# Gram blocks of the eight full chunks in one cluster, and a 16-column product for the meta chunk in the next projection tile's PSUM banks

## The chip, the core and the metric

The kernel runs on one core of a Trainium2 chip. The core has a matrix engine (TensorE, in the profile PE, with its weight loads as PEld), a vector engine (VectorE, DVE), a scalar engine (ScalarE, ACT), GpSimd (POOL), and queues from which transfers are issued (SyncE, SP). Matrix products land in PSUM, which has eight banks of 512 f32 columns on 128 partitions; VectorE and ScalarE move them from there to SBUF. The metric is the device time of one execution in microseconds (us); of several runs the median counts.

## What is computed

One layer of a hybrid encoder on 16 learned meta tokens and 512 real tokens: RMS norm, one input projection, an RWKV-7 recurrence on 16 heads of 64 beside a gated convolution, an output projection, and a final norm. The part that matters here is the recurrence, which is run as a chunk of the 16 meta tokens and eight chunks of 64 tokens.

```python
hn = _rmsnorm(h_res, norm_in_g[l])
P = hn @ w_in[l]                      # 528 x 2048 by 2048 x 8320
...
kk = (k * k_k[l]).reshape(bsz, L, H, N)
kk = kk / jnp.maximum(jnp.linalg.norm(kk, axis=-1, keepdims=True), 1e-12)
...
def step(S, inp):
    r_t, w_t, k_t, v_t, kk_t, b_t = inp
    sa = jnp.einsum('bhvk,bhk->bhv', S, kk_t)
    S = (S * w_t[:, :, None, :]
         - sa[..., None] * b_t[:, :, None, :]
         + v_t[..., None] * k_t[:, :, None, :])
    y_t = jnp.einsum('bhvk,bhk->bhv', S, r_t)
    return S, y_t

S, y_meta = lax.scan(step, S0, tuple(t[:N_META] for t in xs))
S, y_real = lax.scan(chunk_step, S, real)      # chunks of 64
```

The kernel computes a chunk in matrix form. For each chunk and head it needs the products of the chunk's keys (and betas) with its own queries and removal vectors, token against token, masked to the lower triangle: the Gram blocks.

## The kernel before

**Layout.** Channels lie on partitions, tokens along the free dimension. Two heads of 64 channels make a pair; there are eight pairs (0 to 7). The 528 tokens are laid out as nine chunks of 64, where chunk 0 is the meta chunk with 16 real columns and 48 of padding.

**The stream.** The input projection is 65 tiles of 128 output columns. `main` (L354) makes one tile from 16 blocks of weights, as three products each (the high and low halves of a split f32 number), over one or two column ranges of the tokens (`FULL`, `TAIL` with two, `REAL` with one): 96 products of about 256 columns, or 48 of 512. Each range has a PSUM bank of the pool `pm` (tag `main`, four banks), so the tile in work and the one before it hold them between them. When a tile is done, `scaled` (L363) on VectorE moves it out of PSUM.

**The pairs.** `prepare(i)` (L637) makes the operands of a pair, and `invert` (L844) inverts the triangles of two pairs at a time. Their products are small, so they are set between those of the stream: `fill(ns)` (L564) issues stream products worth that many nanoseconds, counted as 0.43 ns a column, before the next small products. This order of TensorE is written out by hand (L101), and the constants stand in `FW` (L43). The other engines' queues are ordered by the framework, from priorities and its own costs: `ahead()` (L596) raises a priority. Transfers that are to be issued later are put on a list by `later` (L545) with a due time that counts the stream's nanoseconds.

**The Gram blocks.** In `prepare`, the stationary operand of a chunk is `bk[hs, c, h : h + 2]` (64 channels of head h, 128 columns: two kinds of 64 tokens), the moving one `ar[hs, c]` (the same 64 channels, 128 columns: removal vectors and queries). So both heads use half of the array's rows each. The products are f32, and each appears in the profile as two records. `gram` (L692) issues both heads of a chunk, `masked` (L701) multiplies finished blocks with the triangle masks on VectorE and writes them to `gt` in SBUF. Before, it goes like this:

- `fill(FW["gram"])`, or `gram_b` for odd pairs (L689)
- a cluster of chunks 0 to 7 (L714): the four first in two banks `za` of the pool `pz` (tag `tz`, two banks), the others in `zc`, in the two single banks `misc` and `ser`
- four masks of 128x512 (L716, L717), then `fill(FW["gram2"])`
- a second cluster: chunk 8 (L721) in two `tz` banks `ze`; then the norm sums (L726, L727: 2 weight columns, 288 moving ones), of which one half lies beside chunk 8 in `ze[0]` and the other in `misc`; then the bonus sums `zb` (L729, L730) in `ser`
- two masks of 128x128 for chunk 8 (L734)

What follows in `prepare` sends the masked blocks through DRAM to the solver of the 16x16 triangles (L753 to L802, on VectorE) and to the operands of the recurrence.

The weights of the stream come by `prefetch` (L162): a transfer on SP's queue, a rounding copy on ScalarE (L158), and a subtraction on VectorE or GpSimd (L159) for the low half. The convolution's tiles (`C`, `h`, `B`, `gc`) use VectorE, ScalarE and GpSimd in turn (L426 to L462).

Of the kernel before, what the change touches and what calls it, by code (L numbers as in the profile page):

```python
# [9 lines left out]
F32 = mybir.dt.float32  # L10
# [3 lines left out]
ALU = mybir.AluOpType  # L14
# [4 lines left out]
P = 128  # L19
# [3 lines left out]
META = 16  # L23
L = SEQ + META
CH = 64
NCH = SEQ // CH + 1
LP = NCH * CH
# [13 lines left out]


FW = dict(  # L43
    evac=34, start=1062, lora=2200, gram=8000, gram_b=13500, gram2=5500, misc=2000, v=2000, vt=1000, solve=24500, more={0: 5500, 2: 2400},
    tr=3200, lev=3000, cp=4200, out=1500, begin=19500, p=2900, u=2900, s=5200, last=3700, mix=2600,
)

# [51 lines left out]
def hymba_kernel(ctx: ExitStack, tc: tile.TileContext, xt, xtok, front, w_in, w_out, pv, lup, cst, msk, gf, out):  # L99
    nc = tc.nc  # L100
# [11 lines left out]
    gmask = cs[:, C_GM : C_GM + 256].rearrange("p (h c) -> p h c", h=2)  # L112
# [14 lines left out]
    plan = [("lora", 0), ("k", 0), ("r", 0), ("B", 0), ("v", 0), ("k", 1), ("r", 1), ("v", 1), ("g", 0), ("g", 1)]  # L127
# [10 lines left out]
    N_IN = len(stream)  # L138
    stream += [w_out[0, g] for g in range(3)]
    quarters, chain, low = {}, {}, {}  # L140
    state = {"next": 0}

# [41 lines left out]
    pm = ph1.enter_context(tc.tile_pool(name="pm", bufs=4, space=PSUM))  # L186
    pz = ph1.enter_context(tc.tile_pool(name="pz", bufs=2, space=PSUM))
    pi = ph1.enter_context(tc.tile_pool(name="pi", bufs=1, space=PSUM))
# [128 lines left out]
    with tc.issue_after(head):  # L317
        nc.vector.tensor_scalar(
            out=omm, in0=pvt[:, V_MU : V_MU + 33], scalar1=-1.0, scalar2=1.0, op0=ALU.mult, op1=ALU.add
# [17 lines left out]
    def steps(ps, ranges, k4, q, ks=range(4), rs_=range(2)):  # L337
        hi, lo = quarters[q]
        for r, (a, b) in enumerate(ranges):
            if r not in rs_:  # L340
                continue
            for k in ks:
                kt = 4 * k4 + k
                w = slice(k * P, (k + 1) * P)
                for n, (ww, xx) in enumerate(((hi, xh), (hi, xl), (lo, xh))):
                    nc.tensor.matmul(  # L346
                        ps[r], ww[:, w], xx[:, kt, a:b], start=(kt == 0 and n == 0), stop=(kt == KT - 1 and n == 2)
                    )
                    yield (b - a) * 0.43

    def banks(ranges, name, pool, tag):
        return [pool.tile([P, b - a], F32, tag=tag, name=f"ps_{name}_{r}") for r, (a, b) in enumerate(ranges)]

    def main(j, ranges, name):  # L354
        prefetch(2 * j + 4)
        ps = banks(ranges, name, pm, "main")
        for k4 in range(4):
            if k4 == 1:
                prefetch(2 * j + 5)
            yield from steps(ps, ranges, k4, 4 * j + k4)  # L360
        return ps

    def scaled(ranges, ps, dst, base):  # L363
# [200 lines left out]
    def fill(ns):  # L564
        while ns > 0:
            seen = len(ready)
            t = step()
            if t is None:
                return
            ns -= t  # L570
            if len(ready) > seen:
                ns += FW["evac"]
# [23 lines left out]
    def ahead():  # L596
        return tc.high_priority(offset=AHEAD)
# [42 lines left out]
    def prepare(i):  # L640
        p = i % 2
# [35 lines left out]
        r = got["r", i]  # L677
# [8 lines left out]
        nc.scalar.activation(sq, k, AF.Square, scale=col(V_KK, i))  # L686
        sqh, sql = split(sq, f"sq{i}", LP)
        rh, rl = split(r, f"rk{i}", SEQ)
        fill(FW["gram_b" if p else "gram"])  # L689

        gt = cq.tile([P, 2, NCH, P], F32, tag=f"gt{p}", name=f"gt{i}")
        def gram(z, c, c0):  # L692
            for h, hs, ho in heads:
                nc.tensor.matmul(  # L694
                    z[h][:, c - c0],
                    bk[hs, c, h : h + 2, :].rearrange("p a s -> p (a s)"),
                    ar[hs, c].rearrange("p a s -> p (a s)"),
                    start=True, stop=True,
                )

        def masked(z, c0, c1):  # L701
            with ahead():
                for h in range(2):
                    nc.vector.tensor_tensor(
                        out=gt[:, h, c0:c1],
                        in0=z[h],
                        in1=gmask[:, h].unsqueeze(1).to_broadcast([P, c1 - c0, P]),
                        op=ALU.mult,
                    )


        za = [pz.tile([P, 4, P], F32, tag="tz", name=f"g{i}_0_{h}") for h in range(2)]
        zc = [pi.tile([P, 4, P], F32, tag=("misc", "ser")[h], name=f"g{i}_4_{h}") for h in range(2)]
        for c in range(8):  # L714
            gram(za if c < 4 else zc, c, c // 4 * 4)
        masked(za, 0, 4)  # L716
        masked(zc, 4, 8)  # L717
        fill(FW["gram2"])

        ze = [pz.tile([P, P + 288 * (1 - h)], F32, tag="tz", name=f"g{i}_8_{h}") for h in range(2)]  # L720
        gram([z[:, 0:P].unsqueeze(1) for z in ze], 8, 8)  # L721
        n2 = tr(f"n2{i}")
        zn = pi.tile([2, 288], F32, tag="misc", name=f"n2_{i}")
        zs = ((zn, 0, 288), (ze[0][0:2, P : P + 288], 288, LP))
        for z, a, b in zs:
            nc.tensor.matmul(z, ones[:, P : P + 2], sqh[:, a:b], start=True, stop=False)  # L726
            nc.tensor.matmul(z, ones[:, P : P + 2], sql[:, a:b], start=False, stop=True)  # L727
# [3 lines left out]
        with ahead():  # L731
            for z, a, b in zs:
                nc.scalar.copy(n2[0:2, a:b], z)
            masked([z[:, 0:P].unsqueeze(1) for z in ze], 8, 9)  # L734
        nc.scalar.copy(r, zb)
        fill(FW["misc"])

# [801 lines left out]
```

## Time and profile before

| what | value |
|---|---|
| three runs | 1003.79, 1004.59, 1004.99 us; median 1004.59 |
| the profiled execution | 1003.5 us, of which the span from its first to its last instruction is 1001.6 |
| mean granted clock of TensorE | 0.997 |
| input projection's products (L346) | starts from about 5 to 839 us of the span |
| Gram products (L694) | 288 records, 20.4 us busy, from 79.4 to 554 us |
| masks (L704) | 32 of 128x512 at 675 ns, 16 of 128x128 at 286 ns |

A row of a group names line, engine, operation, the tiles written and read, the shape and the count; then the busy time in us and the mean ns of one. A row of the timeline gives the start and length in us and the count of like instructions that were merged. PE rows count the matmuls, PEld rows the loads of the stationary operand. Matmuls are pipelined, so a record (here some 0.27 us) is longer than the distance from one start to the next; what a product costs is that distance. A row of a wait names who waited for whom: total us, times, longest.

### The profile page before, as it was taken

What the parts mean: (1) busy time and instruction counts of PE and PEld (TensorE: products, weight loads), DVE (VectorE), ACT (ScalarE), POOL (GpSimd) and SP (SyncE); (2) the same over time, 40 slices, a digit from 0 to 9 for tenths busy, and PEclk for the clock granted to TensorE, in tenths of its full rate; (3) what the DMA queues carried; (4) which work ended last, traced back from release to release, by engine and by line L of the source; (5) the groups of instructions that cost most, each with busy time, mean ns of one, the idle gap of its engine ahead of it and who ended that gap; (6) DMA issues with size and microseconds to landing.
All of it is one profiled execution on the core that took longest, in us unless ns stands there. A gap on an engine that the chain in (4) does not pass through costs nothing.

```text
span 1001.6 us, 23672 instructions
## 1 busy us (share of the span) xinstructions
PE 991.5 (99%) x9723; PEld 913.1 (91%) x9723; DVE 679.7 (68%) x1247; ACT 394.5 (39%) x729; POOL 273.2 (27%) x284
## 2 busy tenths in 40 slices
PE   9999999999999999999999999999999999999996
PEld 8999999999998999998999998989889898888885
DVE  7777865586775569654669654245555697997897
ACT  7553423344323434322434322223232435546454
POOL 0122524234222423233423232223332333001001
PEclk9999999999999999999999999999999999999998
DMA  9426586546675364854263855868674698797654
GB/s 332 144 84 152 126 219 159 153 128 143 154 185 168 99 167 101 216 158 119 85 173 96 224 143 166 321 201 249 203 227 101 171 268 212 187 304 188 160 127 168
DMA packets 185036, 174.82 MB, mean 175 GB/s; under 512 B 121568, under 2 KB 142816, under 8 KB 184416
## 3 DMA queue, kind: packets, MB, share of 16 engines
q1 hardware_dynamic: 182336, 164.40, 56.8%
q0 software_dynamic: 2304, 8.39, 4.9%
q8 instruction: 76, 1.25, 0.5%
q10 hardware_dynamic: 288, 0.52, 0.1%
q14 instruction: 32, 0.26, 0.1%
HBM read 136.92 MB, written 36.35 MB: 173 GB/s over the span
## 4 chain that ended last, share of the span: by engine, by line
PE 95%; DVE 3%; issue 1%; DMA 0%; ACT 0%; DVEq 0%; POOL 0%; ACTq 0%
PE ps_k L346 9%; PE ps_v L346 9%; PE ps_h L346 9%; PE ps_r L346 9%; PE ps_C L346 9%; PE ps_g L346 9%; PE ps_B L346 9%; PE ps_gc L346 9%; PE M L1256 5%; PE P L1256 4%; PE g L694 2%; PE Q L1256 2%; DVE o L1227 1%; PE ps_lora L346 1%; PE zs L1019 1%; PE rz L967 1%
## 5 line engine op out<-in xcount | busy, mean ns | idle before, releaser
L159 POOL TENSOR_TENSOR w<-wr,w 128x512 fp32r<-128x512 f32 x119 | 173.1, 1455 | 367.5 <-ACT w L158 316.3
L158 ACT CAST w<-wr 128x512 fp32r<-128x512 f32 x252 | 153.1, 619 | 287.2 <-PE ps_C L346 48.9
L159 DVE TENSOR_TENSOR w<-wr,w 128x512 fp32r<-128x512 f32 x133 | 98.2, 744 | 107.8 <-ACT w L158 107.5
L346 PE MATMUL ps_k<-xh,w 128*128 128x272 f32 (+1 forms) x512 | 95.3, 284 | 0.0
L346 PE MATMUL ps_v<-xh,w 128*128 128x256 f32 (+1 forms) x512 | 95.3, 284 | 0.0
L346 PE MATMUL ps_r<-xh,w 128*128 128x258 f32 (+1 forms) x512 | 94.9, 281 | 0.0
L346 PE MATMUL ps_h<-xh,w 128*128 128x256 f32 (+1 forms) x512 | 94.2, 283 | 0.0
L346 PE MATMUL ps_C<-xh,w 128*128 128x256 f32 (+1 forms) x512 | 93.1, 281 | 0.0
L346 PE MATMUL ps_g<-xh,w 128*128 128x256 f32 (+1 forms) x512 | 91.5, 280 | 0.0
L346 PE MATMUL ps_B<-xh,w 128*128 128x512 f32 x256 | 83.9, 395 | 0.0
L346 PE MATMUL ps_gc<-xh,w 128*128 128x512 f32 x256 | 81.3, 392 | 0.0
L346 PEld LDWEIGHTS ps_k<-xh,w 128*128 128x128 f32 x512 | 80.0, 188 | 0.4
L346 PEld LDWEIGHTS ps_v<-xh,w 128*128 128x128 f32 x512 | 80.0, 188 | 0.3
L346 PEld LDWEIGHTS ps_h<-xh,w 128*128 128x128 f32 x512 | 79.3, 188 | 0.9 <-issue 0.2
L346 PEld LDWEIGHTS ps_r<-xh,w 128*128 128x128 f32 x512 | 79.9, 188 | 0.1
L346 PEld LDWEIGHTS ps_C<-xh,w 128*128 128x128 f32 x512 | 79.2, 188 | 0.6
L346 PEld LDWEIGHTS ps_g<-xh,w 128*128 128x128 f32 x512 | 78.7, 188 | 0.3
L346 PE MATMUL ps_k<-xl,w 128*128 128x272 f32 (+1 forms) x256 | 72.6, 284 | 0.0
L346 PE MATMUL ps_v<-xl,w 128*128 128x272 f32 (+1 forms) x256 | 72.5, 283 | 0.0
L346 PE MATMUL ps_r<-xl,w 128*128 128x258 f32 (+1 forms) x256 | 72.2, 282 | 0.0
L346 PE MATMUL ps_g<-xl,w 128*128 128x258 f32 (+1 forms) x256 | 72.0, 281 | 0.0
L346 PE MATMUL ps_C<-xl,w 128*128 128x258 f32 (+1 forms) x256 | 71.8, 280 | 0.0
(321 smaller groups left out, 2256.7 us busy)
## 6 DMA issues: line engine op xcount, KB each, us to landing
wr<-in_w_in_dram SPq DMA_DIRECT2D x126, 512.0 KB
ct<-opd SPq DMA_DIRECT2D x64, 288.0 KB
wo<-in_w_out_dram SPq DMA_DIRECT2D x24, 512.0 KB
x<-in_w_out_dram POOLq DMA_DIRECT2D x16, 512.0 KB, 6.1
opd<-ar SPq DMA_DIRECT2D x8, 576.0 KB
opd<-gt SPq DMA_DIRECT2D x16, 288.0 KB
opd<-bt SPq DMA_DIRECT2D x64, 64.0 KB
x<-in_w_out_dram SPq DMA_DIRECT2D x8, 512.0 KB
```

Of the source, the lines that this page charges most:

```text
L158: nc.scalar.copy(hi, rq)
L159: low[q] = eng.tensor_tensor(out=lo, in0=rq, in1=hi.bitcast(F32), op=ALU.subtract).ins
L346: nc.tensor.matmul(ps[r], ww[:, w], xx[:, kt, a:b], start=(kt == 0 and n == 0), stop=(kt == KT - 1 and n == 2))
L694: nc.tensor.matmul(z[h][:, c - c0], bk[hs, c, h : h + 2, :].rearrange("p a s -> p (a s)"), ar[hs, c].rearrange("p a s -> p (a s)"), start= ...
L967: nc.tensor.matmul(z[e][ho if e else hs, 0, k], t[hs, o : o + CH], t[hs, O_V : O_V + CH] if part else st[hs, 4 * e + k], start=(part == 0 ...
L1019: nc.tensor.matmul(d[hs, j], w, x[hs], start=(a == 0), stop=(a == b - 1))
L1227: last = nc.vector.tensor_tensor(out=lo, in0=rq, in1=hi.bitcast(F32), op=ALU.subtract)
L1256: nc.tensor.matmul(bank[s], left(prod, jj, m, s), w, start=(jj == 0 and n == 0), stop=(jj == 7 and n == 2))
```

## The change

The eight full chunks (1 to 8) form one cluster, in the banks that chunks 0 to 7 had. The meta chunk's block is computed only for its 16 real columns and only against the removal vectors (`gram_meta`); the rest of its place in `gt` is set to zero on GpSimd. Its product is put into the two banks that the next projection tile is about to use (`next_banks`); `main` takes these banks over when it starts that tile, so its first product into each waits for the mask that reads the block. It stands before the cluster when more than 48 products of the current projection tile have been issued, after it otherwise. The norm sums lose the bank they shared with chunk 8 and get one of their own. For pair 0 alone the cluster is moved 2000 ns of stream later, and the filler behind it is shortened by as much.

```diff
@@ -41,7 +41,7 @@
 
 
 FW = dict(
-    evac=34, start=1062, lora=2200, gram=8000, gram_b=13500, gram2=5500, misc=2000, v=2000, vt=1000, solve=24500, more={0: 5500, 2: 2400},
+    evac=34, start=1062, lora=2200, gram=8000, meta={0: 2000}, gram_b=13500, gram2=5500, misc=2000, v=2000, vt=1000, solve=24500, more={0: 5500, 2: 2400},
     tr=3200, lev=3000, cp=4200, out=1500, begin=19500, p=2900, u=2900, s=5200, last=3700, mix=2600,
 )
 
@@ -138,7 +138,7 @@
     N_IN = len(stream)
     stream += [w_out[0, g] for g in range(3)]
     quarters, chain, low = {}, {}, {}
-    state = {"next": 0}
+    state = {"next": 0, "step": 0, "banks": []}
 
 
 
@@ -351,13 +351,21 @@
     def banks(ranges, name, pool, tag):
         return [pool.tile([P, b - a], F32, tag=tag, name=f"ps_{name}_{r}") for r, (a, b) in enumerate(ranges)]
 
+    def next_banks():
+        what, i = plan[state["tile"] + 1]
+        return [pm.tile([P, 512], F32, tag="main", name=f"ps_{what}{i}_{r}") for r in range(2)]
+
     def main(j, ranges, name):
         prefetch(2 * j + 4)
-        ps = banks(ranges, name, pm, "main")
+        early = state["banks"]
+        state.update(tile=j, step=0, banks=[])
+        ps = [early[r][:, 0 : b - a] for r, (a, b) in enumerate(ranges)] if early else banks(ranges, name, pm, "main")
         for k4 in range(4):
             if k4 == 1:
                 prefetch(2 * j + 5)
-            yield from steps(ps, ranges, k4, 4 * j + k4)
+            for t in steps(ps, ranges, k4, 4 * j + k4):
+                state["step"] += 1
+                yield t
         return ps
 
     def scaled(ranges, ps, dst, base):
@@ -686,9 +694,10 @@
         nc.scalar.activation(sq, k, AF.Square, scale=col(V_KK, i))
         sqh, sql = split(sq, f"sq{i}", LP)
         rh, rl = split(r, f"rk{i}", SEQ)
-        fill(FW["gram_b" if p else "gram"])
+        fill(FW["gram_b" if p else "gram"] + FW["meta"].get(i, 0))
 
         gt = cq.tile([P, 2, NCH, P], F32, tag=f"gt{p}", name=f"gt{i}")
+        nc.gpsimd.memset(gt[:, :, 0, META:P], 0.0)
         def gram(z, c, c0):
             for h, hs, ho in heads:
                 nc.tensor.matmul(
@@ -697,6 +706,22 @@
                     ar[hs, c].rearrange("p a s -> p (a s)"),
                     start=True, stop=True,
                 )
+
+        def gram_meta():
+            z = next_banks()
+            for h, hs, ho in heads:
+                nc.tensor.matmul(
+                    z[h][:, 0:META],
+                    bk[hs, 0, h : h + 2, :].rearrange("p a s -> p (a s)"),
+                    ar[hs, 0, 0, 0:META],
+                    start=True, stop=True,
+                )
+            with ahead():
+                for h in range(2):
+                    nc.vector.tensor_tensor(
+                        out=gt[:, h, 0, 0:META], in0=z[h][:, 0:META], in1=gmask[:, h, 0:META], op=ALU.mult
+                    )
+            state["banks"] = z
 
         def masked(z, c0, c1):
             with ahead():
@@ -709,19 +734,24 @@
                     )
 
 
-        za = [pz.tile([P, 4, P], F32, tag="tz", name=f"g{i}_0_{h}") for h in range(2)]
-        zc = [pi.tile([P, 4, P], F32, tag=("misc", "ser")[h], name=f"g{i}_4_{h}") for h in range(2)]
-        for c in range(8):
-            gram(za if c < 4 else zc, c, c // 4 * 4)
-        masked(za, 0, 4)
-        masked(zc, 4, 8)
-        fill(FW["gram2"])
-
-        ze = [pz.tile([P, P + 288 * (1 - h)], F32, tag="tz", name=f"g{i}_8_{h}") for h in range(2)]
-        gram([z[:, 0:P].unsqueeze(1) for z in ze], 8, 8)
+        late = state["step"] > 48
+        if late:
+            gram_meta()
+        za = [pz.tile([P, 4, P], F32, tag="tz", name=f"g{i}_1_{h}") for h in range(2)]
+        zc = [pi.tile([P, 4, P], F32, tag=("misc", "ser")[h], name=f"g{i}_5_{h}") for h in range(2)]
+        for c in range(1, NCH):
+            gram(za if c < 5 else zc, c, (c - 1) // 4 * 4 + 1)
+        if not late:
+            gram_meta()
+        masked(za, 1, 5)
+        masked(zc, 5, 9)
+        fill(FW["gram2"] - FW["meta"].get(i, 0))
+
         n2 = tr(f"n2{i}")
-        zn = pi.tile([2, 288], F32, tag="misc", name=f"n2_{i}")
-        zs = ((zn, 0, 288), (ze[0][0:2, P : P + 288], 288, LP))
+        zs = [
+            (pi.tile([2, 288], F32, tag="misc", name=f"n2_{i}"), 0, 288),
+            (pz.tile([2, 288], F32, tag="tz", name=f"n2b_{i}"), 288, LP),
+        ]
         for z, a, b in zs:
             nc.tensor.matmul(z, ones[:, P : P + 2], sqh[:, a:b], start=True, stop=False)
             nc.tensor.matmul(z, ones[:, P : P + 2], sql[:, a:b], start=False, stop=True)
@@ -731,7 +761,6 @@
         with ahead():
             for z, a, b in zs:
                 nc.scalar.copy(n2[0:2, a:b], z)
-            masked([z[:, 0:P].unsqueeze(1) for z in ze], 8, 9)
         nc.scalar.copy(r, zb)
         fill(FW["misc"])
```

## The prediction

> **What bounds the kernel now.** I read the head of the page first, then the chain that ended last, then what TensorE waits for.
>
> ```profile
> span 1001.6 us, 23672 instructions
> PE 991.5 (99%) x9723; PEld 913.1 (91%) x9723; DVE 679.7 (68%) x1247; ACT 394.5 (39%) x729; POOL 273.2 (27%) x284
> ...
> PE 95%; DVE 3%; issue 1%; DMA 0%; ACT 0%; DVEq 0%; POOL 0%; ACTq 0%
> ```
>
> ```profile
> PEld ps_B L346 <- DVE w L159: 0.4, 1, 0.4
> ```
>
> TensorE (PE) sets the time: 95% of the chain is its own matmuls, and the only wait for a projection weight in the whole list of its waits is one of 0.4 us. So a change is worth what it takes out of, or puts between, the starts of consecutive matmuls; work taken off other engines is worth nothing unless PE waits for it. The timeline of PE around the second Gram cluster of pair 0 shows what such a cluster costs.
>
> ```profile
> 87.15 0.28 PE L346 MATMUL ps_r<-xl,w 128*128 128x256 f32 x1
> 87.27 0.28 PE L346 MATMUL ps_r<-xh,w 128*128 128x256 f32 x1
> 87.48 0.49 PE L694 MATMUL g<-ar,bk 64*128 64x128 f32 x4
> 87.90 0.29 PE L726 MATMUL n<-sq_h,ones 128*2 128x288 f32 x1
> ...
> 88.30 0.30 PE L727 MATMUL g<-sq_l,ones 128*2 128x288 f32 x1
> 88.43 0.40 PE L729 MATMUL zb<-rk_h,ones 128*128 128x512 f32 x1
> ```
>
> Projection products follow each other at 0.12 us (87.15 to 87.27). Going from them to the Gram blocks, which use half the rows for each head, takes 0.21 (87.27 to 87.48), and the four records of one chunk plus the way back take 0.42 (87.48 to 87.90). The first cluster has eight chunks.
>
> ```profile
> 79.37 2.06 PE L694 MATMUL g<-ar,bk 64*128 64x128 f32 x32
> 81.35 0.38 PE L346 MATMUL ps_r<-xl,w 128*128 128x256 f32 x1
> ```
>
> ```profile
> L694 PE MATMUL g<-ar,bk x288: 272/272/373, 79.4 to 553.9; 64*128 64x128 f32 x144
> ```
>
> The last of the 32 ends at 79.37 + 2.06 = 81.43 and lasted 0.27, so it started at 81.16; the next projection starts 0.20 later (the way back). The 32 starts span 1.79 us. Four records make two steps (both heads start together, twice, since each f32 product is two records), so there are 16 steps; the first is long (0.2), the others take some 0.11.
>
> **The change part by part.**
>
> *Chunk 8 leaves its own cluster.* Between 87.27 and 87.90 lie 0.63 us; without Gram blocks there the norm product would follow a projection product at the ordinary 0.12. Removed: 0.51 us a pair, 8 pairs, **4.1 us**. What follows (norms, bonus sums) stays as it is. No row shows a projection product directly followed by the two-column norm product. The nearest is the reverse: 88.30 to 88.43, 0.13, is the ordinary step of a 288-column product, with no extra. I take no extra. At the other end stands a drain as in the 0.21 of 87.27 to 87.48, 0.09 more a pair, 0.7 us in all.
>
> [...]
>
> *Chunk 8 joins the first cluster, and the meta chunk becomes 16 columns wide.* The eight full chunks cost what chunks 0 to 7 cost now. The meta chunk is added as two more steps. Does a step of 16 columns cost an eighth? The trace has a product of one column with a full weight tile, the token sums of L471. Two windows of different length on its weight loads, from the same start:
>
> ```profile
> 44.26 0.43 PEld L471 LDWEIGHTS pss<-cs,accd 128*128 128x128 f32 x3
> ```
>
> ```profile
> 44.26 0.99 PEld L471 LDWEIGHTS pss<-cs,accd 128*128 128x128 f32 x8
> ```
>
> Five more loads take 0.56 us, 0.112 each, though each product moves a single column: the load of 128 f32 columns sets the step. The meta block keeps its 128 weight columns (keys and betas of one chunk), so I charge 2 x 0.112 = 0.22 us a pair, **1.8 us** for 8. Bounds: at best only the columns count (2 x 16 x 0.8 ns, the price of a column worked out next, 0.03 a pair; a rival below), at worst 0.112 a step as now.
>
> *The way back gets shorter where the meta block stands last.* The small products of 32 columns show it.
>
> ```profile
> 185.03 0.75 PE L906 MATMUL t<-xm,gt 32*32 32x32 f32 x64
> 185.71 0.39 PE L346 MATMUL ps_r<-xh,w 128*128 128x258 f32 x1
> ```
>
> ```profile
> L906 PE MATMUL t<-xm,gt 32*32 32x32 f32 x256 | 3.0, 194 | 0.0
> ```
>
> The last starts at 185.78 - 0.19 = 185.59, and the projection 0.12 later, against 0.20 after 128 columns: 0.8 ns a column, so 0.11 after 16 and 0.09 saved. Which order a pair gets depends on how many projection steps of the current tile were issued (over 48: meta first). The windows below run from each tile's begin to its cluster; x counts the projection matmuls (one or two of the tile before run in).
>
> ```profile
> core 0: us, PE busy (x) PEld busy (x), PEclk, DMA share, GB/s
> 77.45:79.36 1.91, 1.91 (x17) 1.79 (x16) 1.00 0.69 193
> 116.20:120.83 4.63, 4.63 (x40) 4.51 (x39) 1.00 0.00 0
> 204.30:212.18 7.88, 7.88 (x67) 7.77 (x65) 1.00 0.43 133
> 243.45:253.73 10.28, 10.28 (x89) 10.16 (x87) 1.00 0.43 118
> 342.60:351.27 8.67, 8.67 (x73) 8.55 (x72) 1.00 0.41 125
> 393.25:396.20 2.95, 2.95 (x27) 2.83 (x25) 1.00 0.01 3
> 492.05:500.71 8.66, 8.66 (x73) 8.55 (x72) 1.00 0.34 114
> 542.70:545.65 2.95, 2.95 (x26) 2.83 (x25) 1.00 0.00 0
> ```
>
> Pairs 2, 3, 4 and 6 stand over 48; pairs 0 (16, plus about 18 for the 2000 ns moved), 1, 5 and 7 under it. Four pairs save 0.09: **0.4 us**.
>
> *The banks of the next projection tile.* They were last used by the tile before the current one, so the meta products now wait until VectorE (DVE) has evacuated that tile. Everything on PE stands behind such a wait. Pair 0 and, for the others, pair 5:
>
> ```profile
> 81.88 0.76 DVE L365 TENSOR_TENSOR pr_k<-ps_k,rs 128x272 f32<-128x272 f32 x2
> ...
> 84.26 2.47 DVE L704 TENSOR_TENSOR gt<-g,cs 128x512 f32<-128x512 f32 x4
> ```
>
> ```profile
> 396.26 0.73 DVE L365 TENSOR_TENSOR pr_v<-ps_v,rs 128x272 f32<-128x272 f32 x2
> ```
>
> Pair 0: the banks are free at 82.64. Its cluster, moved 2.0 us later, runs from about 81.4, and the meta products come last, at 83.2: no wait (at the old place, 81.2, it would have been 1.5 us). Moving it moves no DMA; the 2000 ns are taken off the next filler, so the norms and the timed transfers keep their place. Its products then end at 83.4, still ahead of the masks' place in VectorE's queue (84.26). These four end at 86.73, two small ones before them (under 0.3 each) make it 87.3, and the norm product that needs the banks comes at 87.4. Pair 5: banks free at 396.99, meta products at some 396.2 + 0.1 + 1.9 = 398.2. I cost these waits at nothing; without that cover, up to 1 us a pair.
>
> *The next tile waits for the meta masks.* The room is what is left of the current tile: short only in pair 3, whose cluster comes 88 steps into 96.
>
> ```profile
> 256.43 0.38 DVE L365 TENSOR_TENSOR pr_g<-ps_g,rs 128x258 f32<-128x258 f32 x1
> 256.74 0.67 DVE L159 TENSOR_TENSOR w<-wr,w 128x512 fp32r<-128x512 f32 x1
> 257.33 1.87 DVE L704 TENSOR_TENSOR gt<-g,cs 128x512 f32<-128x512 f32 x3
> ```
>
> The cluster starts at 253.74 (the window's end), takes 2.0 + 0.2, and the 8 steps left take 0.9: the next tile is due at about 257.0. If the meta masks run before 256.43, nothing waits; in the place of today's masks, 257.33, the next tile waits 0.5 to 0.9 us. They become ready about a microsecond before the others, since the meta products go first there, so I take 0 and keep 0.9 for the range.
>
> *VectorE and GpSimd.*
>
> ```profile
> L704 DVE TENSOR_TENSOR gt<-g,cs 128x128 f32<-128x128 f32 x16 | 4.5, 286 | 3.1 <-ACT n L733 2.8
> L768 POOL MEMSET y<- 72x256 f32 x8 | 2.5, 308 | 0.0
> L159 POOL TENSOR_TENSOR w<-wr,w 128x512 fp32r<-128x512 f32 x119 | 173.1, 1455 | 367.5 <-ACT w L158 316.3
> ```
>
> Sixteen masks of 286 ns become sixteen of 16 columns, cheaper and off the path. The new memset (224 columns a row) costs about 0.3 us, like that of 256, on a POOL whose weight splits stand idle 367.5 us before they start. Nothing.
>
> **Sum.** 4.1 - 1.8 + 0.4 = **2.7 us less**. The profiled execution took 1003.5 us (span 1001.6 and 1.9 around it), 1.1 below the median of the runs, 1004.59. The sum makes the one 1000.8 and the other 1001.9; I predict **1001.9**.
>
> **Rivals.**
>
> 1. *The next tile waits in pair 3*: 0.9 us, 1002.8. For it: all four big masks run 3.6 us after the cluster's start there, and the room is 3.3. Against: the meta masks are asked for first.
>
> 2. *The norm product is entered through a drain*: 0.7 us, 1002.6. For it: every change to half-row blocks costs 0.2. Against: 88.30 to 88.43. [...]
>
> 3. *The queues are redrawn.* Only PE's order is written by hand; VectorE, ScalarE, GpSimd and the transfers are ordered anew. One place has no room to spare:
>
> ```profile
> 292.20 0.42 DVE L365 TENSOR_TENSOR hh<-ps_h,rs 128x256 f32<-128x256 f32 x1 [0.93 <-PE ps_h L346]
> ...
> 294.80 1.54 DVE L441 SCALAR_TENSOR_TENSOR cv<-u,pvt,cv 128x512 f32<-128x512 f32 x2 [2.17 <-ACT cv L438]
> 296.26 3.48 DVE L159 TENSOR_TENSOR w<-wr,w 128x512 fp32r<-128x512 f32 x2
> ```
>
> These splits feed the products that already waited 0.4 us. The chain starts from PE itself (end of ps_h), so PE's gain shifts all of it; but two more operations ahead of the split (0.8 to 1.7 each) make 1.5 to 3 us of stall: 1003.4 to 1004.9, say 1004.5. Against: the change adds little work, far from there.
>
> 4. *The meta masks stand behind the four big ones (slower).* In pair 3 they then come at 257.33 + 2.47 (the four of pair 0) = 259.8, end at 260.3, and the next tile waits 3.3 us. Pair 2 has more room:
>
> ```profile
> 215.55 2.44 DVE L704 TENSOR_TENSOR gt<-g,cs 128x512 f32<-128x512 f32 x4
> ```
>
> Its cluster starts at 212.18, 65 steps into 96, so the next tile is due at 212.2 + 2.2 + 31 x 0.115 = 218.0; the masks would end at 218.0 + 0.5, 0.5 late. I take the same for pairs 4 and 6. Together 4.8, 2.1 us slower in all: 1006.7. It decides once the waits pass 2.7 us. Against: they come first in the order of the program, at the same priority.
>
> 5. *16 columns are nearly free*: 0.2 us more a pair, 1.6 in all, 1000.3. Against: 0.112 a load in L471.
>
> **How the numbers follow.** Forecast 47% (1001.3 to 1002.5 of its own: part of the drain, half a wait, the spread of the runs), rival 1 13%, 2 9%, 3 19%, 4 6%, 5 6%. The range reaches from rival 5 to the long end of rival 3 with the runs' spread, **1000.3 to 1005.2**, leaving out rival 4 and the tails. About 0.2%, 2.0 us, is what a measurement here can tell from no change. Faster by more (below 1002.6): the forecast, rival 5, some of 1 and 2: 58%. Within: the rest of those and two thirds of 3: 30%. Slower: rival 4 and several stalls like rival 3's at once: 12%.
>
> **What would show it.** In the profile after: no L694 line between projection and norm products, and 0.12 there (0.21: rival 2); clusters of 36 records, 0.22 longer, the narrow ones 0.11 a step (0.01 to 0.03: rival 5); a way back of 0.11 in pairs 0, 1, 5, 7 and 0.20 in 2, 3, 4, 6; no wait of a projection tile for gt's masks (rivals 1, 4) and no new one for w (rival 3). The forecast is wrong if PE's waits grow by over a microsecond, or if the busy time of the narrow products is far from their weight loads.

## The result and the profile after

| | median | lowest to highest | runs |
|---|---|---|---|
| before | 1004.22 us | 1003.35 to 1005.60 | 14 |
| after | 1001.97 us | 1001.06 to 1002.57 | 14 |

The ratio is 0.9979, with a 95% interval of 0.9972 to 0.9986: 2.25 us less. The profiled execution of after took 1002.49 us, its span 1000.7, at a granted clock of 0.997. First the head of its page, with the line of a queue that the page calls `instruction`:

```profile
span 1000.7 us, 23699 instructions
PE 989.0 (99%) x9723; PEld 912.3 (91%) x9723; DVE 684.7 (68%) x1247; ACT 395.3 (39%) x729; POOL 271.2 (27%) x292
...
q8 instruction: 76, 1.25, 0.5%
...
PE 90%; DVE 5%; DMA 2%; issue 1%; SPq 0%; ACT 0%; POOL 0%; DVEq 0%; ACTq 0%; POOLq 0%
```

PE has the same 9723 matmuls and is 2.5 us less busy (991.5 before), but the span is only 0.9 shorter. PE's share of the chain fell from 95% to 90%, yet a second profile of the same kernel has 92%, so this line isn't one to read a microsecond from. The timeline of PE (start, length, engine, line, operation, tiles, shape, count) shows the parts of the change in pair 0, which computes the meta block last, and in pair 3, which computes it first:

```profile
81.91 2.06 PE L703 MATMUL g<-ar,bk 64*128 64x128 f32 x32
83.80 0.30 PE L713 MATMUL ps_v<-ar,bk 64*128 64x16 f32 x4
84.03 0.39 PE L346 MATMUL ps_r<-xl,w 128*128 128x258 f32 x1
...
87.81 0.28 PE L346 MATMUL ps_r<-xh,w 128*128 128x256 f32 x1
87.92 0.29 PE L756 MATMUL n<-sq_h,ones 128*2 128x288 f32 x1
...
253.07 0.40 PE L713 MATMUL ps_g<-ar,bk 64*128 64x16 f32 x4
253.32 2.04 PE L703 MATMUL g<-ar,bk 64*128 64x128 f32 x32
255.28 0.39 PE L346 MATMUL ps_g<-xl,w 128*128 128x256 f32 x1
```

The second cluster is gone: from the last projection product (87.81) to the norm product (87.92) it is 0.11 us, where 0.63 lay before. The first cluster has its four narrow records at one end. Their weight loads keep the wide ones' pace: in pair 3 the two loads for a head's narrow block start at 253.07 and 253.18, the first load for a wide one at 253.29, 0.11 a step. Measured in ns from the start of the last projection product to the start of the first one behind the cluster, it takes 2326 to 2328 in pairs 0, 1, 5 and 7 and 2414 in 2, 3, 4 and 6, against 2191 to 2197 before: 0.13 us and 0.223 us more. The norm product is entered after 113 to 126 ns in the eight pairs. So the steps gain 8 x 0.51 - 4 x 0.13 - 4 x 0.223 = **2.7 us**.

To see where the time went I laid the starts of the 5472 projection products of the two profiles side by side, first to first and so on. The difference falls by 0.514 behind each of the eight norm sums and grows by 0.131 or 0.223 at each cluster, and stands at -2.3 us when the last pair is done. It began at +0.4, before the first Gram product, where PE waits for operands of the first tiles; the same product before and then after:

```profile
8.70 0.39 PE L346 MATMUL ps_lora<-xl,w 128*128 128x272 f32 x1
```

```profile
9.14 0.39 PE L346 MATMUL ps_lora<-xl,w 128*128 128x272 f32 x1 [0.22 <-DVE xl L228]
```

What ScalarE makes for these products starts when a transfer of the first operands has landed (L227), at 7.11 and 6.96 us in two profiles of the kernel before and at 7.55 and 7.38 in two of the change. Side by side, the change is 0.3 to 0.6 us behind there, so the start is one place where time can be lost. Then, at 758 us, far from everything that the change touches, the difference jumps back by 1.2 us, of which 1.0 is left once the longer step of before, four products further on, is passed too. The waits of PE name the place, as total us, times, longest:

```profile
PE ps_h L346 <- issue: 1.0, 1, 1.0
```

"issue" means that PE waited for nothing that the profile shows. The timeline of PE there, after and then before:

```profile
756.39 0.38 PE L346 MATMUL ps_h<-xh,w 128*128 128x256 f32 x1
757.81 0.39 PE L346 MATMUL ps_h<-xl,w 128*128 128x256 f32 x1 [1.04 <-issue]
```

```profile
759.07 0.28 PE L346 MATMUL ps_h<-xl,w 128*128 128x256 f32 x1
759.34 0.50 PE L346 MATMUL ps_h<-xh,w 128*128 128x256 f32 x2
```

Both stand shortly behind the dense products of one chunk of the recurrence. After, PE stops for 1.42 us (756.39 to 757.81) at the second projection product behind them. Before, the first product behind them starts at 758.50, and it is the step to the sixth that is longer than its neighbours (759.07 to 759.34, 0.27 where 0.12 is ordinary). I count the rows of PE and PEld (matmuls, weight loads, and the wait instructions among them) from the span's start: both stops stand at the same place, between row 16,832 and row 16,834. After has 96 wait instructions on PE where before has 88, so eight rows more come ahead of that place, and since a projection product is two rows (load and matmul), the place falls four products earlier.

What takes up part of the 2.7 us had to be settled, then. **The theory of the stop**: the stop belongs to a fixed place of PE's stream, near row 16,833, and not to the products that stand there; the change moved that place four products nearer to the dense cluster, so that PE comes to it earlier, and if it goes on at the same time as before, this gives back 4 x 0.115 = 0.5 us (an estimate from the ordinary step), whatever else the change does. **Its rival**: the stop is chance or noise of one run and the lost time lies in the Gram part itself (waits for banks and masks, a product that costs other than its loads). Each of the first experiments takes one part of the change by itself; the last ones move the stop. None of them is made to test the loss at the start.

### The profile page after: what moved, and what is told of

Read it like the earlier page. It is cut to its first block, busy times and chain, and to the rows that moved or that the text cites. A ratio compares the mean times of both kernels' runs of the same rounds, so it can differ in the third digit from the quotient of the medians.

```text
span 1000.7 us, 23699 instructions
## 1 busy us (share of the span) xinstructions
PE 989.0 (99%) x9723; PEld 912.3 (91%) x9723; DVE 684.7 (68%) x1247; ACT 395.3 (39%) x729; POOL 271.2 (27%) x292
## 3 DMA queue, kind: packets, MB, share of 16 engines
q8 instruction: 76, 1.25, 0.5%
## 4 chain that ended last, share of the span: by engine, by line
PE 90%; DVE 5%; DMA 2%; issue 1%; SPq 0%; ACT 0%; POOL 0%; DVEq 0%; ACTq 0%; POOLq 0%
PE ps_v L346 9%; PE ps_k L346 9%; PE ps_h L346 9%; PE ps_g L346 9%; PE ps_r L346 9%; PE ps_B L346 9%; PE ps_gc L346 9%; PE ps_C L346 8%; PE M L1285 5%; PE P L1285 2%; DVE o L1256 2%; PE g L703 2%; PE Q L1285 1%; PE ps_lora L346 1%; PE zs L1048 1%
## 5 line engine op out<-in xcount | busy, mean ns | idle before, releaser
L159 POOL TENSOR_TENSOR w<-wr,w 128x512 fp32r<-128x512 f32 x119 | 170.7, 1436 | 343.7 <-ACT w L158 290.9
L346 PE MATMUL ps_h<-xl,w 128*128 128x258 f32 (+1 forms) x256 | 71.9, 281 | 1.0 <-issue 1.0
```

The costliest lines, as they stand in the source:

```text
L159: low[q] = eng.tensor_tensor(out=lo, in0=rq, in1=hi.bitcast(F32), op=ALU.subtract).ins
L346: nc.tensor.matmul(ps[r], ww[:, w], xx[:, kt, a:b], start=(kt == 0 and n == 0), stop=(kt == KT - 1 and n == 2))
```

## The experiments

Where an edit is shown, it is against the changed kernel. Medians stand beside the runs of the kernel before on the same chip: 1003.86 us in the first four (31 runs) and the next four (22 runs), 1003.96 in the last three (15 runs).

**1. The change once more**, unedited.

> The changed kernel itself, a second time. The profiled execution of the first look lost 0.4 us before 9 us (first weights) and 1.2 us at one place at 757 us, where PE waited for nothing that the profile shows; step by step the change took 2.66 us off. If both losses are chance, this profile shows no such gap at 757 us and a span nearer to 999.4; if the gap belongs to the changed order of instructions, it comes again at the same product. Either way: eight clusters of 36 records, 2.33 us from the last projection product before to the first after where the meta block is last, 2.41 where it is first, and 0.12 into the norm products.

1001.49 us, ratio 0.9977 (0.9967 to 0.9986), 2.37 us less. The clusters take the same 2.33 and 2.41. PE stops at the same product again, and this time its step is 0.73 us over the ordinary one, against 1.30 in the first profile. So the place is fixed and the length varies.

**2. The meta block 128 columns wide**, with all else as in the change.

```diff
-        nc.gpsimd.memset(gt[:, :, 0, META:P], 0.0)
-                    z[h][:, 0:META],
+                    z[h][:, 0:P],
-                    ar[hs, 0, 0, 0:META],
+                    ar[hs, 0].rearrange("p a s -> p (a s)"),
-                        out=gt[:, h, 0, 0:META], in0=z[h][:, 0:META], in1=gmask[:, h, 0:META], op=ALU.mult
+                        out=gt[:, h, 0], in0=z[h][:, 0:P], in1=gmask[:, h], op=ALU.mult
```

> The meta chunk's block is computed over all 128 columns, as the others, in the same banks and at the same place; the memset goes and the small masks are 128x128. If a step costs its load of 128 weight columns (my account), only the way back grows, where the meta block is last: 2.41 us in all eight clusters, 4 x 0.09 = 0.35 us more than the changed kernel, about 1002.3. If 16 columns are nearly free (the rival), each pair loses 0.2: 1.6 us more, 1003.6, and clusters of 2.41 against 2.2 or less.

1002.18 us, 0.9983 (0.9974 to 0.9992). The timeline of PE in pair 0:

```profile
81.97 2.06 PE L702 MATMUL g<-ar,bk 64*128 64x128 f32 x32
83.86 0.39 PE L712 MATMUL ps_v<-ar,bk 64*128 64x128 f32 x4
84.18 0.39 PE L346 MATMUL ps_r<-xl,w 128*128 128x258 f32 x1
```

From the cluster's first row to the next projection product: 2.21 us, against 2.12 with 16 columns (84.03 - 81.91). The clusters take 2.42 in pairs 0, 1, 5 and 7, and an unaltered 2.414 where the meta block stands first. So eight times fewer columns save 0.093 us in the four pairs where the block stands last, and nothing where it stands first: 0.37 us, too little for these medians (0.7 between the two kernels, intervals overlapping). The rival that 16 columns are nearly free falls.

**3. The meta block first in all pairs.**

```diff
-        late = state["step"] > 48
+        late = True
```

> The meta block always stands ahead of the eight chunks. The way back is 0.20 in all pairs: 0.35 us more. The banks of the next tile must then be free at the cluster's start: in the profile of the changed kernel they are free at 83.1 in pair 0 (cluster at 81.9), at 120.9 in pair 1 (cluster at 120.9), and long before in the others. So PE waits 1.2 us in pair 0, about 0.1 in pair 1: 1.6 us slower than the changed kernel, some 1003.6. If the wait for the banks is nothing, 0.35 slower.

1003.86 us, 1.0000 (0.9992 to 1.0009): the whole gain is gone. The timeline of PE in pair 0:

```profile
81.56 0.40 PE L346 MATMUL ps_r<-xh,w 128*128 128x258 f32 x2
82.79 0.68 PE L713 MATMUL ps_v<-ar,bk 64*128 64x16 f32 x3 [0.83 <-DVE pr_k L373]
...
85.39 0.39 PE L346 MATMUL ps_r<-xl,w 128*128 128x258 f32 x1
```

The block waits for VectorE, which still moves the tile before out of the first bank, and then for the second bank; the cluster takes 3.71 us, 1.38 more. In pair 1 I had expected 0.1 and it is 0.96: VectorE comes to the old tile later there than I had worked out from its place in pair 1 of the changed kernel. A line of PE's waits has it, the one wait that isn't in pair 0:

```profile
PE ps_C L713 <- DVE pr_g L373: 0.4, 1, 0.4
```

So the order by the 48 products is worth 2.3 us in two pairs.

**4. Pair 0 without its 2000 ns.**

```diff
-    ... gram=8000, meta={0: 2000}, gram_b=13500, ...
+    ... gram=8000, meta={}, gram_b=13500, ...
```

> Pair 0's cluster is not moved by 2000 ns. My step said that its meta products would wait 1.5 us for the banks of tile k1 (free at 82.6 to 83.1, products due at 81.2 to 81.7): 1.5 us slower than the changed kernel, 1003.5, with the wait in pair 0 alone. The rival: VectorE's queue is ordered anew and evacuates that tile earlier, and nothing is lost.

1003.36 us, 0.9996 (0.9987 to 1.0005). The timeline of PE in pair 0:

```profile
78.90 2.06 PE L703 MATMUL g<-ar,bk 64*128 64x128 f32 x32
81.89 0.72 PE L713 MATMUL ps_v<-ar,bk 64*128 64x16 f32 x4 [0.94 <-DVE pr_k L373]
82.55 0.39 PE L346 MATMUL ps_r<-xl,w 128*128 128x256 f32 x1
```

The wait is back: this cluster takes 3.85 us instead of 2.33. The 1.52 us between them is the 1.5 that the prediction gave for the old place.

**5. The meta block by itself ahead of the norm sums**, 16 columns wide, in the banks that it had before: the half of the change that narrows, without the half that joins.

```diff
-            z = next_banks()
+            z = [pz.tile([P, META], F32, tag="tz", name=f"g{i}_0_{h}") for h in range(2)]
-            state["banks"] = z
-        late = state["step"] > 48
-        if late:
-            gram_meta()
-        if not late:
-            gram_meta()
         n2 = tr(f"n2{i}")
+        gram_meta()
```

> Chunks 1 to 8 form the first cluster; the 16-column meta block stands alone where the second cluster was, just ahead of the norm products, in two banks of the pool tz. So the products are those of the changed kernel and only their grouping differs. If a change between projection and half-row blocks is what costs, each pair pays again 0.21 + 0.22 + 0.11 = 0.54 before its norms in place of 0.12, and its first cluster shrinks to 2.19 (from 2.33 or 2.41): 8 x 0.42 - 4 x 0.14 - 4 x 0.22 = 1.9 us more than the changed kernel, 1003.6. If the gain came from the narrower product and lighter masks, the time stays near 1001.7.

1003.91 us, 1.0002 (0.9993 to 1.0010): narrowing without joining, in these banks, gains nothing in the time. The timeline of PE in pair 0, and a line of PE's waits:

```profile
86.84 0.28 PE L346 MATMUL ps_r<-xh,w 128*128 128x256 f32 x1
87.05 0.40 PE L713 MATMUL g<-ar,bk 64*128 64x16 f32 x4
87.37 0.29 PE L751 MATMUL n<-sq_h,ones 128*2 128x288 f32 x1
87.50 0.29 PE L752 MATMUL n<-sq_l,ones 128*2 128x288 f32 x1
87.70 0.29 PE L751 MATMUL n2b<-sq_h,ones 128*2 128x288 f32 x1
```

```profile
PE n2b L751 <- DVE gt L721: 0.4, 1, 0.4
```

A change of shape and four narrow records put 0.53 us (86.84 to 87.37) in the place of 0.12. Against the change that is 0.35 to 0.42 a pair and 0.75 in pair 3, 3.3 in all by the side-by-side starts. This is more than I had worked out, since I had given the second norm sum a bank that the meta block holds: it comes 0.07 late in pair 0 (0.20 from 87.50 to 87.70 where 0.13 is ordinary) and waits 0.4 in pair 3. The medians differ by 2.4; part of the rest may be the stop at 758 us, which is shorter here (0.28 over the ordinary step, against 1.30 and 0.73). So this run shows what the join is worth together with the second norm sum's bank, not the join alone.

**6. The meta block with 80 weight columns instead of 128**: the 64 tokens of one kind and the 16 that aren't padding of the other; the rest of the block is set to zero.

```diff
-        nc.gpsimd.memset(gt[:, :, 0, META:P], 0.0)
+        nc.gpsimd.memset(gt[:, :, 0], 0.0)
-                    z[h][:, 0:META],
-                    bk[hs, 0, h : h + 2, :].rearrange("p a s -> p (a s)"),
+                    z[h][0:80, 0:META],
+                    bk[hs, 0, h : h + 2, :].rearrange("p a s -> p (a s)")[:, 0:80],
-                        out=gt[:, h, 0, 0:META], in0=z[h][:, 0:META], in1=gmask[:, h, 0:META], op=ALU.mult
+                        out=gt[0:80, h, 0, 0:META], in0=z[h][0:80, 0:META], in1=gmask[0:80, h, 0:META], op=ALU.mult
```

> The meta block takes 80 of its 128 weight columns (all 64 of one kind, the 16 real ones of the other); the rows left out are zero by the memset. If the load of weight columns sets the step (0.83 ns a column), each load that nothing hides is 0.04 shorter: one where the block is last (2.33 to 2.29), two where it is first (2.41 to 2.33), 0.5 us less than the changed kernel in all. If a narrow step has a floor of its own, the clusters stay 2.33 and 2.41.

1001.46 us, 0.9975 (0.9966 to 0.9985). The timeline of PE in pair 2:

```profile
211.85 0.32 PE L713 MATMUL ps_r<-ar,bk 64*80 64x16 f32 x4
212.02 2.03 PE L703 MATMUL g<-ar,bk 64*128 64x128 f32 x32
```

The clusters take 2.284 and 2.334 us, 0.04 and 0.08 less, as expected. Here it is the weight columns that were cut, and now the steps do get shorter: from the first narrow record to the first wide one 0.17 us, against 0.25 in pair 3 of the change (253.07 to 253.32). With run 2 this shows what a narrow block costs: where it stands first, its loads count (0.08 for 48 weight columns) and the columns that move don't (2.414 with 16 and with 128); where it stands last, both do (0.04 for 48 weight columns, 0.093 for 112 moving ones). Over 8 pairs the 80 columns save 0.5 us, which the medians can't show.

**7. 80 weight columns, and the meta block last in all pairs but 3.** To run 6 this adds

```diff
-        late = state["step"] > 48
+        late = state["step"] > 80
```

> As the 80-column version, and the meta block stands last in all pairs but 3 (bound 80 in place of 48): clusters of 2.29 in seven pairs, 0.6 us less than the changed kernel. Pairs 2, 4 and 6 then leave the next tile 2.7 to 3.5 us for the masks; if these come 1 us after the cluster, as in pairs 0 and 1 at the latest, 3.5 to 4, PE waits there for the masks and the gain is lost.

1000.72 us, 0.9970 (0.9959 to 0.9981), 3.1 us less than before and the lowest median of all versions. Seven clusters take 2.28 us. The danger was that the next tile waits for the masks; the timelines of PE and of VectorE around pair 2 show that it doesn't:

```profile
211.34 2.06 PE L703 MATMUL g<-ar,bk 64*128 64x128 f32 x32
213.22 0.25 PE L713 MATMUL ps_r<-ar,bk 64*80 64x16 f32 x4
213.41 0.50 PE L346 MATMUL ps_k<-xh,w 128*128 128x256 f32 x2
...
217.20 0.28 PE L346 MATMUL ps_r<-xh,w 128*128 128x258 f32 x1
```

```profile
216.47 0.15 DVE L721 TENSOR_TENSOR gt<-ps_r,cs 80x16 f32<-80x16 f32 x1
...
217.15 0.15 DVE L721 TENSOR_TENSOR gt<-ps_r,cs 80x16 f32<-80x16 f32 x1
```

The meta product ends the cluster at 213.2, VectorE comes to its masks three microseconds later; the first ends at 216.6 and the second at 217.3. The next tile's first product, into the first of the two banks, starts at 217.20 at the ordinary step, so PE goes on without a wait, with 0.6 us to spare. By steps this version gains 0.7 us on the change (3 x 0.136 for the pairs that change their order, 0.08 in pair 3, 4 x 0.043 in the others). The ratios, 0.9970 beside 0.9977 and 0.9979 of the change, leave 0.7 to 0.9 us, but their intervals overlap, so how far it beats the change isn't settled by the times.

**8. The kernel before once more**, for one execution.

> The kernel before, for a second profile. In its first profile PE loses 0.26 us between its records 16832 and 16836 (two steps of 0.27 and 0.23 in place of 0.12), at 759 us; the changed kernel, with eight more wait instructions on PE, loses 0.5 to 1.4 us at the same count of records, which there is the second product behind a dense cluster and here the fifth. If the loss hangs on the place in PE's instruction stream, it is again small here, about 0.5 less than in the changed kernel; if it is chance, it can be anything.

1003.63 us, span 1001.7. (The count in this expectation is off by one: in the first profile of before, too, it is the sixth product behind the cluster.) The timeline of PE:

```profile
758.57 0.28 PE L346 MATMUL ps_h<-xl,w 128*128 128x256 f32 x1
759.47 0.50 PE L346 MATMUL ps_h<-xh,w 128*128 128x256 f32 x2 [0.62 <-issue]
```

The stop stands at the same product as in the first profile of before, and lasts 0.78 over the ordinary step instead of 0.16. So the kernel before has it as well; it is not made by the change. Its length varies there as much as in the change (0.6 us between two profiles of one kernel).

**9. Eight more rows on PE, ahead of everything**: the two warm-up products of 512 columns become four of 256 (each of these is two matmul records with a load each, so eight rows come in), which leaves the Gram part as it is.

```diff
-    for _ in range(2):
-        nc.tensor.matmul(pwarm, cold[:, 0:P], cold, start=True, stop=True)
+    for n in range(4):
+        nc.tensor.matmul(pwarm[:, 0:256], cold[:, 0:P], cold[:, 0:256], start=True, stop=True)
```

> The changed kernel with its two warm-up products of 512 columns cut into four of 256: the same time on PE before the first weights arrive, 8 more PE records in the stream. In nine profiles so far PE stops at the same count of its records, between 16832 and 16834, whichever product that is, and goes on some 1.4 us after the end of one transfer of instructions. If the place in the stream decides, the stop comes four products earlier: at the end of the dense cluster of the recurrence, ahead of or at the first projection product behind it, and no shorter (0.7 us or more). If it hangs on the products themselves, it stays at the second projection product.

1003.9 us, span 1002.1, in one execution. The timeline of PE:

```profile
755.98 0.22 PE L1052 MATMUL zy<-u,ct 64*64 64x64 f32 x1
758.21 0.33 PE L1052 MATMUL zy<-u,ct 64*64 64x64 f32 x3 [2.02 <-issue]
```

The stop has moved from behind the dense cluster into it, to row 16,834 again, and is the longest of all: 2.2 us. Nothing at that place was edited. Beside the first profile of the change, the projection products are level at 9 us (0.02 later) and lose 1.0 us more at the stop.

**10. Four rows fewer**: one warm-up product.

```diff
-    for _ in range(2):
+    for n in range(1):
```

> The changed kernel with one warm-up product in place of two: 4 PE records fewer. By the place in the stream the stop moves two products later, to the fourth projection product behind the dense cluster, and is about 0.23 us shorter (some 0.4 to 1.0 us). What the missing warm-up costs at the start (before 9 us) is read apart from that. If it hangs on the products, it stays at the second.

1003.67 us, span 1001.9, in one execution. The timeline of PE:

```profile
758.21 0.28 PE L346 MATMUL ps_h<-xh,w 128*128 128x256 f32 x1
758.87 0.39 PE L346 MATMUL ps_h<-xh,w 128*128 128x256 f32 x1 [0.38 <-issue]
```

The stop moves the other way, to the fourth product, and lasts 0.54. But the first projection products, some 20 from 5.5 us on, run 0.1 us slower each than in the change, and 1.1 to 1.2 us of that stays (beside its two profiles): this execution is slower than the change.

**11. Runs 7 and 10 together.**

> The 80-column version with the meta block last in seven pairs, and one warm-up product: 4 records fewer than that version. The stop moves to two products later and shrinks by about 0.23 us; if the start costs nothing, 0.2 us less than the version with both warm-up products (1000.7), which is under what can be told; if the start is slower for want of warm-up, up to 1 us more.

1002.10 us, 0.9980 (0.9971 to 0.9989). The stop comes at the fifth product and is down to 0.18, but the start loses 1.6. So shortening the stop in this way costs more than the stop; run 7 has the lowest median, though its interval overlaps with this one.

The stop in all profiles, by the product behind the dense cluster at which it falls, as the step's length over the ordinary 0.12 us:

| at product | rows against the changed kernel | stop, us |
|---|---|---|
| sixth | 8 fewer (before, run 8), 9 fewer (run 5) | 0.16, 0.78, 0.28 |
| fifth | 6 fewer (run 11) | 0.18 |
| fourth | 4 fewer (runs 3, 10) | 0.64, 0.54 |
| third | 2 fewer (run 7) | 0.62 |
| second | as many (the change, runs 1, 2, 4, 6) | 1.30, 0.73, 1.00, 1.27, 1.34 |
| inside the cluster | 8 more (run 9) | 2.2 |

Runs 3, 5 and 7 have fewer wait instructions on PE (92, 87 and 94 instead of 96), since their products stand in another order; run 11 has both these and fewer products. Two rows move the stop by one product, in both directions, whether they are waits of the Gram part or warm-up products 750 us earlier. So the theory of the stop holds for its place, and against the rival the clusters and norm sums show no loss of their own. The length falls from about 1.1 us at the second product to some 0.4 at the sixth (means of the rows of the table); with a spread of 0.6 in one kernel, that it falls by what the products take is not shown.

## Why the prediction was right, and where it wasn't

The median, 1001.97 us, is 0.1 above the predicted 1001.9. By its steps:

- **"Removed: 0.51 us a pair, 8 pairs, 4.1 us."** Measured 0.514 a pair in the side-by-side starts. The norm product follows at 0.113 to 0.126 us, where rival 2 had 0.21. So it falls in all eight pairs. What the prediction and that rival call a drain is the measured step of 0.21 in place of 0.12 on the way from a projection product to half-row blocks (87.27 to 87.48 before); no run shows what PE does in it.
- **"2 x 0.112 = 0.22 us a pair, 1.8 us"** and **"four pairs save 0.09"**. Measured 0.223 where the block stands first and 0.13 where it stands last, so 1.4 in all, as 1.8 - 0.4. The row of L471, a product of one column with a full weight tile, was the right one to price a narrow block by where its load isn't hidden; run 2 (columns) and run 6 (weights) show it from both sides. Rival 5 falls. The sign that the prediction gave for the 0.09 did not come, though: the way back in pairs 0, 1, 5 and 7 is 0.19 us from the start of the last narrow record to the projection product, not 0.11. What got shorter is mostly the step between the two narrow products of a head (in the records of pair 0, 0.03 us from start to start, and 0.11 with 128 columns in run 2). The row of L906, from which the 0.11 was worked out, has only 32 weight columns as well as 32 moving ones, and run 6 shows that weight columns shorten the way back too (to 0.15 with 80). So the sum of this term is right, its place is not.
- **"I cost these waits at nothing"**, the banks of the next tile. No product of L713 waits in after. Runs 3 and 4 show what the cover is worth: 1.38 and 0.96 in pairs 0 and 1 by the wrong order, 1.52 in pair 0 at the old place.
- **"I take 0 and keep 0.9 for the range"**, the meta masks in pair 3. Right, with little room. In the timeline of VectorE:

```profile
255.77 0.24 DVE L721 TENSOR_TENSOR gt<-ps_g,cs 128x16 f32<-128x16 f32 x2
255.93 0.68 DVE L159 TENSOR_TENSOR w<-wr,w 128x512 fp32r<-128x512 f32 x1
256.53 1.28 DVE L729 TENSOR_TENSOR gt<-g,cs 128x512 f32<-128x512 f32 x2
```

  The masks (L721) run before the four big ones, as argued, and end at 256.01; the tile's eight last products end their starts at 256.22, and the next tile begins one step later, 0.3 us after the masks. Rivals 1 and 4 fall. In pair 0, where the prediction had the small masks ahead of the four big ones, one comes behind three of them and the other behind all four (ending at 87.97); there the tile has time, since the next one begins at 92.4.
- **Rival 3, the queues are redrawn.** They are: in pair 5 VectorE moves the old tile out of its banks at 392.81 where it was 396.26. That, and the place that the rival named, cost nothing: the 0.4 us of ps_B is unchanged. But in the first profile a new wait for weights, of 0.6 us, stands at 9 us, ahead of all Gram products, at the place where both profiles of the change are 0.3 to 0.6 us behind. Run 4, which differs from the change in one number for pair 0's cluster at about 80 us, is 0.5 to 0.6 us ahead of the kernel before at that place, and run 6 is 0.6 to 0.8 behind; so it looks like the execution and not the change, but no run settles it. The moved tile of pair 5 in the timeline of VectorE:

```profile
392.81 0.77 DVE L373 TENSOR_TENSOR pr_v<-ps_v,rs 128x272 f32<-128x272 f32 x2
```

- **"Nothing"**, the small masks and the memset. In the groups of after: 160 ns a mask (132 to 169 over all) where 286 stood, and 287 ns a memset; PE's waits name none of them.

```profile
L721 DVE TENSOR_TENSOR gt<-ps_g,cs 128x16 f32<-128x16 f32 x6 | 0.9, 160 | 0.0
```

```profile
L700 POOL MEMSET gt<- 128x224 f32 x8 | 2.2, 287 | 16.9 <-ACT sqx L235 7.4 <-PE t L935 5.1 <-PE prs L498 4.3
```

What it left out: **"Sum. 4.1 - 1.8 + 0.4 = 2.7 us less"** took every start saved on PE for time saved at the end. The sum itself is right to the rounding (2.7 measured in the steps), but the medians fell by 2.25 and 2.37. One candidate for the rest is shown in its place: PE stops at a fixed row of its stream (16,832 to 16,834), and the eight additional wait instructions of the change bring this row four products nearer to the dense cluster. If the stop ends when it would have ended before, that is 0.5 us, and 2.7 - 0.5 = 2.2. The other candidate is the start, where the two profiles of the change are 0.3 to 0.6 us behind. How the missing 0.3 to 0.4 us of the medians divides between them is open.

The 0.5 is worked out from the products, not measured by itself. The stop is 1.30 and 0.73 us long in two profiles of the change and 0.16 and 0.78 in two of before, so the means differ by 0.55 and the single values by as much as that within one kernel. A version of the change with eight rows taken out and nothing else altered was not tried (run 10 takes out four, and the start pays for it).

That the predicted time was met as closely as 0.1 us is luck in part. The prediction subtracted the 2.7 from 1004.59, the median of three runs, and the fourteen have 1004.22: a base 0.4 too high made up for a gain 0.4 too large. The runs of after also lie 1.5 us apart.

## What to carry to other kernels

Where a matrix engine's queue sets the time, price a product by the distance between starts, and a narrow one by its weight load: in these clusters, cutting the moving columns from 128 to 16 gained 0.09 us where the narrow block stands last and nothing where it stands first; cutting the weight columns from 128 to 80 gained 0.04 and 0.08. The small group of products of another shape cost mostly its changes of shape here (0.63 us for four records, of which some 0.2 each for the entry and the way back), so look whether such a group can join one of the same shape, if the banks for it are free by then; where they weren't, two pairs lost as much as the change gains in all (2.3 us in run 3). Lay the starts of like products of the two profiles side by side before explaining a total: it showed the gain arriving step by step, and losses at the start and 200 us behind the last edited product.

## What the runs showed of the hardware

**A stop at a fixed row of PE's instructions.** In every profile here PE stops at row 16,832 to 16,834 of its rows, for 0.2 to 2.2 us, inside a dense cluster of 64-column products or shortly behind it (in run 9 four of them start every 0.06 us at 753.8). I set the packets of the queue q8, `instruction` on the page, beside these stops: 76 packets of 16.4 KB, 1.25 MB in all. In all 13 profiles PE goes on between 1.26 and 1.58 us after the end of the last packet ahead of it (after: packet from 755.38 to 756.26, PE at 757.81; before: 756.90 to 757.88, PE at 759.34; run 9: 754.69 to 756.77, PE at 758.21), and these packets take 0.88 to 2.09 us. What PE waits for there is not shown: the profile names no releaser ("issue"), and no run changed these packets by themselves. Wait instructions count as rows here: with eight more of them in the change than before (96, 88) the stop came four products earlier.

**Slower first products with half the warm-up.** With one warm-up product in the place of two, which leaves PE idle for 1.58 us ahead of the first real ones, some 20 products cost 0.1 us more each (run 10: 0.22 from start to start, 7.48 to 7.70, where the change has 0.12; run 11 has the same). With the full warm-up there are such slow products too, but none to eight of them, varying from profile to profile (eight in runs 2 and 9). The timeline of PE in run 10, and in the change:

```profile
5.10 1.25 PE L513 MATMUL ps_lora<-xh,w 128*128 128x272 f32 x4 [1.58 <-ACT xh L227]
...
7.48 0.41 PE L346 MATMUL ps_k<-xl,w 128*128 128x256 f32 x1
7.70 0.41 PE L346 MATMUL ps_k<-xh,w 128*128 128x256 f32 x1
```

```profile
6.58 0.28 PE L346 MATMUL ps_k<-xl,w 128*128 128x256 f32 x1
6.70 0.28 PE L346 MATMUL ps_k<-xh,w 128*128 128x256 f32 x1
```
